# Four of the 32 groups of the samples' cache products on GpSimd and ScalarE, with a new plan, in a decoder layer on one Trainium2 core

## The chip, the core and the metric

The kernel runs on one core of one Trainium2 chip. The metric is the time of one execution on the device in microseconds (us). In the profile PE is TensorE's matrix products, PEld its weight loads, DVE VectorE, ACT ScalarE, POOL GpSimd, and SP SyncE, which issues most of the DMAs. L1223 is line 1223 of the kernel before; an arrow `a<-b` is read "a is written from b".

## What is computed

One step of a hybrid decoder layer for 1024 prompt tokens and 8 samples that share the weights, in float32, with model width 1024, 4 memory heads of width 256, and 256 memory rows. The part that matters here is the cross attention: the prompt attends to a memory whose keys and values are computed in the step, while each of the 8 samples attends to keys and values of its own, which are read from caches.

```python
def layer(x, ...):
    ...
    x = x + concat(pool_mixer(...), conv_mixer(...)) @ w_out
    x = x + cross_attn(rmsnorm(x, g_attn), mk, mv, w_q, w_o)
    h = rmsnorm(x, g_ffn)
    x = x + (silu(h @ w_gate) * (h @ w_up)) @ w_down

def cross_attn(h, k, v, w_q, w_o):
    q = (h @ w_q).reshape(B, L, MEM_HEADS, MEM_HEAD_DIM)
    s = einsum('blhd,bmhd->bhlm', q, k) / sqrt(MEM_HEAD_DIM)
    p = softmax(s, axis=-1)
    o = einsum('bhlm,bmhd->blhd', p, v).reshape(B, L, D_MODEL)
    return o @ w_o
...
xp, hp, cp = layer(xp, zp, zc, 0, mk, mv, *shared)
xs, hs, cs = layer(xs, state_pool[l], state_conv[l], PAST_LEN, cache_mem_k[l], cache_mem_v[l], *shared)
```

## The kernel before

Activations lie with channels on the 128 partitions and the 1024 + 8 = 1032 tokens as columns. Each float32 product is made of three passes: every operand is split into a high half and a residue, and high times high, high times residue and residue times high are summed. A split takes a copy to the rounded type (on ScalarE or GpSimd, L466 or L468) and a subtraction for the residue (on VectorE or GpSimd, L477). So each result that feeds another product costs two instructions on the engines beside TensorE; where the result comes from TensorE's output memory these are the evictions: a copy by ScalarE (L1188 for the value product) and the residue by VectorE (L1189).

The layer runs in stages: the input projections, pooling and convolution with the memory's keys and values (up to some 200 us), the output projection and queries (to 350 us), the attention of four heads (to some 425 us), its output projection `po` (L582), the gated feed-forward with `pr` (L1429) from some 524 us, and the down projection with the final norm.

In the attention stage a prompt block runs through scores `sc` (L1126), maximum and scaled exponential `probs` (L1134, L1136, L1143), normalising (L1151), a transpose `pt` to `pT` (L1165, L1169, L1170), and the value product `pv` into `oo` (L1184, L1188, L1189). `oo0` to `oo7` are the eight halves of the heads' outputs, the 8 sample columns of each included; `po` sums over them. A `po` block takes its 1032 columns in three spans of 344; the samples are the last columns of the last span.

Samples have a key and a value matrix each, so they get no matrix product with the cache: `s_dots` lays one head's query of all samples (`sbcache_k`, broadcast to 128 partitions by a DMA from the scratch `qd`) beside the cache (`spcache_k`), and VectorE multiplies 128x256 and sums it in one instruction for each sample (L1223). Four samples make a group, with one entry in the list of tasks. There are 32 groups: keys and values, 4 heads, 2 halves of 128, 2 sets of four samples. A group's number is 16 for values plus 4 times the head plus 2 times the half plus the set of samples. After a head's key groups come a transpose `ss` (L1236), a softmax on 8 rows (`sst`, `prow`), a DMA to the scratch `pd` and its broadcast `sbcache_v`; then the value groups sum into `qs`, whose halves are written into the sample columns of `oo` (L466 or L468, L477).

Nothing is issued in the order in which it is written. Each step is entered by `add` with the engines that may run it and a cost for each; `order` then plays through the engines, the buffers and the port that VectorE and GpSimd share, takes at each moment the step that can start first (within `SLACK`, by priority), and so fixes the sequence of each engine. `NUDGE` shifts the priority of single steps, `CHOSEN` binds a step to one engine, `LEAD` and `MARGINS` shift loads and costs. On the chip each engine then runs its sequence strictly in order, waiting for the others by semaphores.

Of the kernel before, what the change touches and what calls it, by code (L numbers as in the profile page):

```python
# [1986 lines left out]
```

## Time and profile before

| what | value |
|---|---|
| three runs | 1146.84, 1144.37, 1144.47 us; median 1144.47 us |
| the profiled execution | 1144.27 us |
| its span | 1142.5 us, so 1.8 us lie around it |
| granted TensorE clock, mean | 0.997 of full speed |
| busy: TensorE, VectorE, ScalarE, GpSimd | 1120.8, 927.6, 499.7, 287.8 us |

The busy time of a group of instructions doesn't say what it costs the whole; what ends an engine's idle time does. In a row of the groups by form the number behind x is the count, then stand the busy time in us and the mean of one in ns, and behind the second bar the idle time of that engine just before and what ended it. In a row of the timeline stand the start, the duration, engine, line, operation and operands, and in square brackets the idle time ahead of it with what ended it. Consecutive instructions of a form are joined with their count.

### The profile page before, as it was taken

The numbers are of one execution on the slowest core, as the hardware profiler recorded it, in microseconds if no ns is written. First come the engines' busy times: TensorE is split into PE (matmuls) and PEld (weight loads), VectorE is DVE, ScalarE is ACT, GpSimd is POOL, SyncE is SP. The second block draws the span as 40 slices with busy tenths as digits, with TensorE's granted clock in tenths as the row PEclk, the third lists the DMA queues.
The fourth block names the chain that finished last, engine by engine and source line by source line (L and its number), as shares of the span: only waits on it lengthen the run. The fifth ranks groups of instructions, "written<-read, shape, count | busy, mean of one in ns | idle before, by whom it ended". The sixth has DMA issues, their size and how long they took to land.

```text
span 1142.5 us, 19533 instructions
## 1 busy us (share of the span) xinstructions
PE 1120.8 (98%) x7736; PEld 1067.4 (93%) x7736; DVE 927.6 (81%) x1514; ACT 499.7 (44%) x706; POOL 287.8 (25%) x327
## 2 busy tenths in 40 slices
PE   9999999999999989999999999999999999999996
PEld 8999988999999979999999999999999999999996
DVE  7999999776257886888888888988888798879744
ACT  7766648353243452445233333333433443332444
POOL 2689772133712201433000000000000123332011
PEclk9999999999999999999999999999999999999999
DMA  8444587433485687322424352254433697657612
GB/s 307 94 93 110 127 233 237 163 114 149 165 249 176 207 325 244 123 82 75 140 84 149 128 190 105 100 176 159 156 124 112 237 374 286 242 169 235 186 59 91
DMA packets 66252, 193.54 MB, mean 169 GB/s; under 512 B 8368, under 2 KB 12144, under 8 KB 64880
## 3 DMA queue, kind: packets, MB, share of 16 engines
q1 hardware_dynamic: 62128, 178.81, 43.8%
q0 software_dynamic: 3600, 13.13, 6.6%
q8 instruction: 61, 1.00, 0.4%
q10 hardware_dynamic: 432, 0.36, 0.1%
q14 instruction: 31, 0.25, 0.1%
HBM read 147.84 MB, written 44.43 MB: 168 GB/s over the span
## 4 chain that ended last, share of the span: by engine, by line
PE 78%; DVE 15%; DMA 4%; issue 1%; ACT 1%; POOL 0%; DVEq 0%; SPq 0%; ACTq 0%; POOLq 0%
PE pr L1429 49%; PE po L582 7%; DVE cacc L783 6%; PE ps L582 5%; PE fd L1800 4%; PE oa L582 4%; PE ob L582 4%; DVE spcache_k L1223 1%; PE vps L1027 1%; DMA spcache_k<-in_cache_k 1%; PE kps L949 1%; PE pv L1184 1%; DVE spcache_v L1223 1%; DVE xss L513 1%; DVE x L1854 1%
## 5 line engine op out<-in xcount | busy, mean ns | idle before, releaser
L1429 PEld LDWEIGHTS pr<-ab,wTb 128*128 128x128 f32 x1056 | 123.4, 190 | 2.3 <-issue 0.5
L1429 PE MATMUL pr<-ab,wTa 128*128 128x260 f32 x1056 | 124.9, 275 | 0.0
L1429 PE MATMUL pr<-ab,wTb 128*128 128x260 f32 x1056 | 124.3, 275 | 0.0
L1429 PEld LDWEIGHTS pr<-ab,wTa 128*128 128x128 f32 x1056 | 123.1, 190 | 1.3
L1429 PE MATMUL pr<-ab,wG 128*128 128x512 f32 x528 | 121.1, 380 | 0.0
L1429 PEld LDWEIGHTS pr<-ab,wG 128*128 128x128 f32 x528 | 96.9, 189 | 12.5 <-issue 0.5
L582 PE MATMUL ps<-xop,w 128*128 128x344 f32 x720 | 105.5, 309 | 0.0
L582 PEld LDWEIGHTS ps<-xop,w 128*128 128x128 f32 x720 | 105.0, 189 | 0.0
L1445 DVE TENSOR_TENSOR su<-pr,su 128x520 f32<-128x520 f32 (+1 forms) x112 | 77.3, 692 | 25.9 <-PE pr L1429 25.4
L1429 PEld LDWEIGHTS pr<-hb,dV 128*128 128x128 f32 x768 | 92.3, 190 | 2.2
L1429 PE MATMUL pr<-hb,dV 128*128 128x260 f32 x768 | 92.7, 275 | 0.0
L582 PE MATMUL ps<-xq,w 128*128 128x344 f32 x576 | 87.0, 310 | 0.0
L582 PE MATMUL po<-oo,w 128*128 128x344 f32 x576 | 84.7, 309 | 0.0
L582 PEld LDWEIGHTS po<-oo,w 128*128 128x128 f32 x576 | 84.3, 189 | 0.2
L582 PEld LDWEIGHTS ps<-xq,w 128*128 128x128 f32 x576 | 84.2, 189 | 0.1
L783 DVE SCALAR_TENSOR_TENSOR cacc<-glu,vec,cacc 128x502 f32<-128x502 f32 (+14 forms) x116 | 77.5, 739 | 0.1
L1429 PE MATMUL pr<-hb,dW 128*128 128x512 f32 x288 | 69.2, 379 | 0.0
L1456 POOL MEMSET su<- 128x16 f32 x22 | 2.4, 112 | 255.7 <-PE pr L1429 200.1
L1800 PE MATMUL fd<-ho,w 128*128 128x260 f32 (+1 forms) x432 | 64.3, 311 | 0.0
L1800 PEld LDWEIGHTS fd<-ho,w 128*128 128x128 f32 x432 | 59.8, 190 | 4.4 <-issue 0.5
L1445 DVE TENSOR_TENSOR x<-pr,x 128x512 f32<-128x512 f32 (+1 forms) x76 | 52.3, 690 | 12.7 <-PE pr L1429 11.6
L766 POOL TENSOR_TENSOR y<-y,cp 128x511 f32<-128x511 f32 (+14 forms) x46 | 57.6, 1254 | 14.9 <-DVE y L766 7.2
(314 smaller groups left out, 2164.7 us busy)
## 6 DMA issues: line engine op xcount, KB each, us to landing
gr<-in_w_gu SPq DMA_DIRECT2D x44, 512.0 KB, 3.4
hb<-su SPq DMA_DIRECT2D x16, 520.0 KB, 3.8
hb<-hb SPq DMA_DIRECT2D x16, 520.0 KB, 6.7
dr<-in_w_dn SPq DMA_DIRECT2D x16, 512.0 KB, 4.0
hb<-bh SPq DMA_DIRECT2D x14, 520.0 KB, 3.3
hb<-hb SPq DMA_DIRECT2D x14, 512.0 KB, 7.4
spcache_k<-in_cache_k SPq DMA_DIRECT2D x12, 512.0 KB, 5.2
ho<-hd SPq DMA_DIRECT2D x10, 520.0 KB, 6.3
```

Of the source, the lines that this page charges most:

```text
L513: add({"Pool": pool_tt(n), "DVE": dve(n)}, lambda e: e.tensor_tensor(total(), total(), sq[:, i, :n], ALU.add), [(sq, i), tkey], [tkey], lo ...
L582: e.matmul(placed(ps[:, c, :CW]), w[:, wi, cols], turns(x[:, xi, c * CW : (c + 1) * CW]), start=first and p == 0, stop=last and p == 2)
L766: add({"Pool": pool_tt(HALF), "DVE": dve(HALF)}, lambda e: e.tensor_tensor(yb[:, i, HALF + n : SEQ], yb[:, i, HALF + n : SEQ], cp[:, q, : ...
L783: e.scalar_tensor_tensor(acc[h][:, n:], src[:, : HALF - n], w, acc[h][:, n:], ALU.mult, ALU.add)
L949: e.matmul(placed(ps[:, 0, i * NMEM : (i + 1) * NMEM]), w[:, wi, block_cols(k)], turns(memg[k // 4][:, xi, k % 4]), start=(k == 0 and p == ...
L1027: e.matmul(placed(ps[:, m]), memg[k // 4][:, xi, k % 4, m * P : (m + 1) * P], turns(w[:, wi, col : col + 512]), start=(k == 0 and p == 0), ...
L1184: e.matmul(placed(ps[:, c]), v[:, vi, m, col : col + P], turns(pT[h][m][:, pi, sl]), start=(m == 0 and p == 0), stop=(m == 1 and p == 2))
L1223: e.scalar_tensor_tensor(piece[:, b], piece[:, b], 1.0, bc[:, b], ALU.mult, ALU.mult, accum_out=out(m)[:, first + b : first + b + 1])
L1429: e.matmul(placed(bank(c)), w[:, wi, cols(j)], turns(xs[0](j, xi)[:, c * n : (c + 1) * n]), start=onto is None and j == 0 and p == 0, stop ...
L1445: from_sums(sums, "DVE", dve, lambda e, src, sl: e.tensor_tensor(as_banks(o(sl), src), src, as_banks(a(sl), src), op), [akey], [okey])
L1800: e.matmul(placed(view(i)), w[:, wi, col : col + P], turns(hops[k][:, xi, half, lo - half * HALF + i * width // count : lo - half * HALF + ...
L1854: add({"DVE": dve(n * width)}, lambda e, i=i, n=n: e.tensor_tensor(x2[j][:, i : i + n, sl], x2[j][:, i : i + n, sl], fin[:, sl].unsqueeze( ...
```

## The change

Four groups are named in `AWAY`. 13 and 15 are the second four samples of the last head's keys (halves 0 and 1), 29 and 31 those of its values. In them GpSimd multiplies all four samples in one 128x1024 instruction (`times`), and ScalarE sums each sample by a copy with an accumulator (`total`), four instructions. The other 28 groups stay on VectorE. The normalising of probabilities may now run on ScalarE too, and one value product (`pv4`) makes both its column halves before either is copied. All tables of the planner have new numbers, so the order moves all over the program. TensorE and SyncE have the same work as before. Line numbers in the kernel after are higher by about 85 to 110.

```diff
-LEAD = {"w_k": 4, "w_v": 7, "w_out_a": 16, "w_q": 42, "w_in": 22, "w_out_b": 11, "w_o": 14}
+LEAD = {"w_k": 4, "w_v": 7, "w_out_a": 10, "w_q": 34, "w_in": 16, "w_out_b": 12, "w_o": 14}
...
-DOWN_BY_DMA = (0, 0, 0, 4)
+DOWN_BY_DMA = (0, 0, 0, 3)
...
+AWAY = (13, 15, 29, 31)
+PV_MS = ()
+PV_FIRST = (4,)
 SCORES_MM = (5, 12, 13, 15)
-SLACK = {"Pool": 0.021, "ACT": 0.186, "DVE": 0.095, "PE": 0.044}
+SLACK = {"Pool": 0.02, "ACT": 0.109, "DVE": 0.058, "PE": 0.038}
...
 NUDGE = {
-    16: 148, 47: -35, 55: 6, 69: -37, 109: -90, 116: -39, 157: 141, 161: 1316, 177: 49, 178: 49, 179: 49, 180: 49, 181: 49, 182: 49,
+    16: -8, 22: -24, 32: 39, 44: -18, 50: -16, 51: 23, 55: -29, 57: -42, 69: -26, 88: 54, 93: 46, 99: 37, 100: -55, 103: -34, 109:
...
@@ normalise, in the softmax of the prompt's scores
         def normalise(e):
             for i in range(2):
-                e.tensor_scalar(pr[:, 2 * i2 + i], pr[:, 2 * i2 + i], st[:, 6 + i : 7 + i], 1.0, ALU.mult, ALU.mult)
-
-        add({"Pool": 0.95, "DVE": 0.53}, normalise, [(st, 2), (pr, i2)], [(pr, i2)], lock=True)
+                at, factor = pr[:, 2 * i2 + i], st[:, 6 + i : 7 + i]
+                if e is nc.scalar:
+                    e.activation(at, at, AF.Copy, scale=factor)
+                else:
+                    e.tensor_scalar(at, at, factor, 1.0, ALU.mult, ALU.mult)
+
+        add({"Pool": 0.95, "DVE": 0.53, "ACT": 2 * act(NMEM, ptrs=1)}, normalise, [(st, 2), (pr, i2)], [(pr, i2)], lock=True)
@@ pv
+        for step, c in ((matmuls, 0), (matmuls, 1), (copies, 0), (copies, 1)) if n in PV_FIRST else ((matmuls, 0), (copies, 0), (matmuls, 1), (copies, 1)):
+            step(c)
@@ s_dots
-                    add({"DVE": 1.4}, emit, [(piece,), (bc,)], [(piece, part), okey + (m, (first + part) // 4)], lock=True)
+                    dkey = okey + (m, (first + part) // 4)
+                    if number * 4 + m * 2 + (first + part) // 4 not in AWAY:
+                        add({"DVE": 1.4}, emit, [(piece,), (bc,)], [(piece, part), dkey], lock=True)
+                        continue
+
+                    def times(e, part=part, piece=piece, bc=bc):
+                        at = slice(part, part + 4)
+                        e.tensor_tensor(piece[:, at], piece[:, at], bc[:, at], ALU.mult)
+
+                    def total(e, m=m, first=first, part=part, piece=piece):
+                        for b in range(part, part + 4):
+                            e.activation(piece[:, b], piece[:, b], AF.Copy, accum_out=out(m)[:, first + b : first + b + 1])
+
+                    add({"Pool": pool_tt(1024)}, times, [(piece,), (bc,)], [(piece, part)], lock=True)
+                    add({"ACT": 4 * act(256) + 0.8}, total, [(piece, part)], [(piece, part), dkey])
```

The first place is VectorE at the last head's keys, second samples (`k3_0_4`, `k3_1_4`), where it makes the residues of `oo5`, `oo0` and `oo2` from the value products `pv` and those of the transposed probabilities `pT3`. Before:

```order
L1189 TENSOR_TENSOR oo5_4254<-pv5_4236,oo5_4254 128x512
L1223 SCALAR_TENSOR_TENSOR spcache_k3_0_4_4234,ssc_79<-spcache_k3_0_4_4234,sbcache_k3_4_4247 128x256 x4
L1189 TENSOR_TENSOR oo0_3726<-pv0_4283,oo0_3726 128x512
L1223 SCALAR_TENSOR_TENSOR spcache_k3_1_4_4252,ssc_79<-spcache_k3_1_4_4252,sbcache_k3_4_4247 128x256 x4
L1189 TENSOR_TENSOR oo2_3908<-pv2_4304,oo2_3908 128x512
L1244 TENSOR_REDUCE sst3_4331<-ss3_4327 8x1
L1245 SCALAR_TENSOR_TENSOR sst3_4331<-sst3_4331,r16_77 8x1
L1189 TENSOR_TENSOR oo0_3726<-pv0_4283,oo0_3726 128x512
L1170 TENSOR_TENSOR pT3_1_4279<-pt3_2_4294,pT3_1_4279 128x512
```

Now:

```order
L1283 TENSOR_TENSOR oo2_4059<-pv2_4229,oo2_4059 128x512
L1283 TENSOR_TENSOR oo5_4299<-pv5_4282,oo5_4299 128x512
L1257 TENSOR_TENSOR pT3_1_4277<-pt3_2_4294,pT3_1_4277 128x512
L1283 TENSOR_TENSOR oo0_3726<-pv0_4301,oo0_3726 128x512
L1283 TENSOR_TENSOR oo5_4299<-pv5_4282,oo5_4299 128x512
L1283 TENSOR_TENSOR oo0_3726<-pv0_4301,oo0_3726 128x512
L1257 TENSOR_TENSOR pT3_0_4237<-pt3_1_4324,pT3_0_4237 128x512
```

At the same place ScalarE makes the copies of these products; before, there stood only copies and the exponential `prow3` of the samples' softmax. Now:

```order
L1282 ACTIVATE oo5_4299<-pv5_4282 128x512
L1256 ACTIVATE pT3_1_4277<-pt3_2_4294 128x512
L1282 ACTIVATE oo0_3726<-pv0_4301 128x512
L1334 ACTIVATE spcache_k3_0_4_4220,ssc_79<-spcache_k3_0_4_4220 128x256 x4
L1282 ACTIVATE oo5_4299<-pv5_4282 128x512
L1282 ACTIVATE oo0_3726<-pv0_4301 128x512
L1334 ACTIVATE spcache_k3_1_4_4247,ssc_79<-spcache_k3_1_4_4247 128x256 x4
L1256 ACTIVATE pT3_0_4237<-pt3_1_4324 128x512
L1282 ACTIVATE oo6_4370<-pv6_4351 128x512
L1359 ACTIVATE prow3_4389,sst3_4379<-ss3_4367,sst3_4379,r16_77 8x256
```

The eight dots are gone from between VectorE's residues. On ScalarE the four sums of `k3_0` and of `k3_1` stand in front of the second copies of `oo5` and `oo0` and in front of the last copy to `pT3`.

The second place is TensorE at the end of the first two output blocks, `po0` and `po4`, where the samples' values are read (x9 is all three spans, x6 the first two, x3 the last, in which the samples are). Before:

```order
L582 MATMUL po0_4369<-oo7_4427,w44_4075 128x344 x6
L582 MATMUL po4_4491<-oo0_3726,w45_4005 128x344 x9
L582 MATMUL po4_4491<-oo1_3728,w45_4005 128x344 x9
L582 MATMUL po4_4491<-oo2_3908,w45_4005 128x344 x9
L582 MATMUL po4_4491<-oo3_3933,w45_4005 128x344 x9
L582 MATMUL po4_4491<-oo4_4132,w45_4005 128x344 x9
L582 MATMUL po0_4369<-oo6_4374,w44_4075 128x344 x3
L582 MATMUL po0_4369<-oo7_4427,w44_4075 128x344 x3
L582 MATMUL po4_4491<-oo5_4254,w45_4005 128x344 x9
L582 MATMUL po4_4491<-oo6_4374,w45_4005 128x344 x9
```

Now:

```order
L665 MATMUL po0_4359<-oo7_4459,w44_4077 128x344 x6
L665 MATMUL po4_4490<-oo0_3726,w45_4004 128x344 x3
L665 MATMUL po4_4490<-oo1_3877,w45_4004 128x344 x9
L665 MATMUL po4_4490<-oo2_4059,w45_4004 128x344 x9
L665 MATMUL po4_4490<-oo3_3999,w45_4004 128x344 x9
L665 MATMUL po4_4490<-oo4_4145,w45_4004 128x344 x9
L665 MATMUL po4_4490<-oo5_4299,w45_4004 128x344 x9
L665 MATMUL po4_4490<-oo6_4370,w45_4004 128x344 x6
L665 MATMUL po4_4490<-oo7_4459,w45_4004 128x344 x6
L665 MATMUL po0_4359<-oo6_4370,w44_4077 128x344 x3
L665 MATMUL po4_4490<-oo6_4370,w45_4004 128x344 x3
L665 MATMUL po0_4359<-oo7_4459,w44_4077 128x344 x3
```

The last spans of `oo6` and `oo7` have moved behind all other work of `po0` and `po4`.

The third place is GpSimd from the last head's probabilities on (`oo4` to `oo7`: the halves of the samples' columns). Before:

```order
L1151 TENSOR_SCALAR probs3_4077<-probs3_4077,sm3_2_4112 128x256 x2
L1151 TENSOR_SCALAR probs3_4077<-probs3_4077,sm3_1_4156 128x256 x2
L1151 TENSOR_SCALAR probs3_4077<-probs3_4077,sm3_3_4216 128x256 x2
L468 TENSOR_SCALAR oo4_4132<-qs_78 128x8
L477 TENSOR_TENSOR oo4_4132<-qs_78,oo4_4132 128x8
L477 TENSOR_TENSOR oo5_4254<-qs_78,oo5_4254 128x8
L468 TENSOR_SCALAR oo7_4427<-qs_78 128x8
L477 TENSOR_TENSOR oo7_4427<-qs_78,oo7_4427 128x8
```

Now:

```order
L1238 TENSOR_SCALAR probs3_4074<-probs3_4074,sm3_3_4191 128x256 x2
L1330 TENSOR_TENSOR spcache_k3_0_4_4220<-spcache_k3_0_4_4220,sbcache_k3_4_4240 128x1024
L1330 TENSOR_TENSOR spcache_k3_1_4_4247<-spcache_k3_1_4_4247,sbcache_k3_4_4240 128x1024
L551 TENSOR_SCALAR oo4_4145<-qs_78 128x8
L551 TENSOR_SCALAR oo5_4299<-qs_78 128x8
L560 TENSOR_TENSOR oo5_4299<-qs_78,oo5_4299 128x8
L1330 TENSOR_TENSOR spcache_v3_0_0_4194<-spcache_v3_0_0_4194,sbcache_v3_0_4462 128x1024
L1330 TENSOR_TENSOR spcache_v3_1_0_4289<-spcache_v3_1_0_4289,sbcache_v3_0_4462 128x1024
L560 TENSOR_TENSOR oo6_4370<-qs_78,oo6_4370 128x8
```

Four products of 128x1024 with the caches now stand between the probabilities and the columns of `oo6`. On VectorE the dots of `v3_0` and `v3_1` are x4 each where they were x8, and the residue of the weight `w44` stands ahead of the residue of `oo1`'s second half where GpSimd had it.

More of the change, by code (lines that the diff above doesn't have):

```diff
@@ L41 @@
 ORDER = (
[5 rows of a table removed]
[5 rows of a table added]
 )
-BY_DMA = {"w_in": (0, 3, 4, 6, 7, 9, 10, 11), "w_k": (2, 3, 5), "w_o": (4, 5, 6), "w_out_a": (1,), "w_out_b": (3,), "w_q": (4, 5, 6), "w_v": (0, 7), "w_dn": (18, 19), "w_dn2": (1,)}
+BY_DMA = {"w_in": (0, 1, 3, 4, 6, 7, 9, 10, 11), "w_k": (2, 3, 5), "w_o": (4, 5, 6), "w_out_a": (1,), "w_out_b": (3,), "w_q": (4, 5, 6), "w_v": (0, 7), "w_dn": (18, 19), "w_dn2": (1,)}
 WIDE = ("w_k", "w_v")
-LEAD = {"w_k": 4, "w_v": 7, "w_out_a": 16, "w_q": 42, "w_in": 22, "w_out_b": 11, "w_o": 14}
+LEAD = {"w_k": 4, "w_v": 7, "w_out_a": 10, "w_q": 34, "w_in": 16, "w_out_b": 12, "w_o": 14}
 LAST_SPANS = ((0, 512), (512, 260), (772, 260))
@@ L60 @@
 PE_FIXED, PE_COLUMN = 0.0135, 0.000417
+AWAY = (13, 15, 29, 31)
+PV_MS = ()
+PV_FIRST = (4,)
 SCORES_MM = (5, 12, 13, 15)
-SLACK = {"Pool": 0.021, "ACT": 0.186, "DVE": 0.095, "PE": 0.044}
+SLACK = {"Pool": 0.02, "ACT": 0.109, "DVE": 0.058, "PE": 0.038}
 MARGINS = {
     "early": {"PE": (0.93, 0.0), "DVE": (0.93, 0.0), "Pool": (1.01, 0), "ACT": (1.02, 0)},
-    "gated": {"Pool": (1.04, 0.04), "DVE": (1.01, 0.02), "PE": (0.95, 0.04), "ACT": (1.08, 0.06)},
+    "gated": {"Pool": (0.96, 0.04), "DVE": (1.01, 0.02), "PE": (0.95, 0.04), "ACT": (1.1, 0.04)},
     "down": {"DVE": (1.03, 0.103)},
-    "last": {"PE": (0.99, 0), "DVE": (1.02, 0.183)},
+    "last": {"PE": (1.08, 0), "DVE": (1.04, 0.243)},
 }
 NUDGE = {
[45 rows of a table removed]
[116 rows of a table added]
 }
@@ L120 @@
     "ACT": (
-        133, 179, 183, 207, 297, 502, 608, 660, 738, 907, 1374, 1406, 1578, 1617, 1647,
[4 rows of a table added]
     ),
     "DVE": (
-        26, 176, 404, 412, 477, 601, 609, 737, 745, 922, 1395, 1529, 2551, 2552, 2644, 2646,
[4 rows of a table added]
     ),
     "Pool": (
-        141, 184, 186, 198, 206, 388, 409, 415, 419, 520, 529, 539, 541, 555, 651, 654, 661, 664, 718, 719, 721, 725, 906, 1018, 1022,
-        1082, 1095, 1180, 1531, 1648, 2553,
[5 rows of a table added]
     ),
@@ L1174, in pv, with matmuls, emit, copies @@
         h, dt = n // 2, n % 2
-        ps = mm_buf(f"pv{n}", 2)
+        apart = [ms_buf(f"pv{n}_{c}") for c in range(2)] if n in PV_MS else []
+        ps = None if apart else mm_buf(f"pv{n}", 2)
         col, v = (h % 2) * 256 + dt * P, vv[h // 2]
         oo = oop[n]
-        for c in range(2):
+        at = lambda c: apart[c] if apart else ps
+        bank = lambda c: apart[c][:] if apart else ps[:, c]
+        def matmuls(c):
             sl = slice(c * 512, (c + 1) * 512)
-            def emit(e, c=c, sl=sl):
+            def emit(e):
                 for m in range(2):
                     for p, (vi, pi) in enumerate(PASSES):
-                        e.matmul(placed(ps[:, c]), v[:, vi, m, col : col + P], turns(pT[h][m][:, pi, sl]),
+                        e.matmul(placed(bank(c)), v[:, vi, m, col : col + P], turns(pT[h][m][:, pi, sl]),
                                  start=(m == 0 and p == 0), stop=(m == 1 and p == 2))
-            add({"PE": pe(512, 6)}, emit, [(v, 0), (v, 1)] + [(pT[h][m], p, c) for p in range(2) for m in range(2)], [(ps,)])
-            add({"ACT": act(512, True)}, lambda e, c=c, sl=sl: e.activation(halves(oo[:, 0, sl]), drawn(ps[:, c]), AF.Copy), [(ps,)], [(oo, 0, c)])
-            add({"DVE": dve(512)}, lambda e, c=c, sl=sl: e.tensor_tensor(halves(oo[:, 1, sl]), drawn(ps[:, c]), halves(f32(oo[:, 0, sl])), ALU.subtract),
-                [(ps,), (oo, 0, c)], [(oo, 1, c)])
+            add({"PE": pe(512, 6)}, emit, [(v, 0), (v, 1)] + [(pT[h][m], p, c) for p in range(2) for m in range(2)], [(at(c),)])
+        def copies(c):
+            sl = slice(c * 512, (c + 1) * 512)
+            add({"ACT": act(512, True)}, lambda e: e.activation(halves(oo[:, 0, sl]), drawn(bank(c)), AF.Copy), [(at(c),)], [(oo, 0, c)])
+            add({"DVE": dve(512)}, lambda e: e.tensor_tensor(halves(oo[:, 1, sl]), drawn(bank(c)), halves(f32(oo[:, 0, sl])), ALU.subtract),
+                [(at(c),), (oo, 0, c)], [(oo, 1, c)])
+        for step, c in ((matmuls, 0), (matmuls, 1), (copies, 0), (copies, 1)) if n in PV_FIRST else ((matmuls, 0), (copies, 0), (matmuls, 1), (copies, 1)):
+            step(c)
     def s_query(h):
```

182 rows, old and new, of tables (CHOSEN, NUDGE, ORDER) are left out of this document.

## The prediction

> **What bounds the kernel now.** I read the page first, then busy time by stretches, then the waits of TensorE, and only then single instructions.
>
> ```profile
> span 1142.5 us, 19533 instructions
> ...
> PE 1120.8 (98%) x7736; PEld 1067.4 (93%) x7736; DVE 927.6 (81%) x1514; ACT 499.7 (44%) x706; POOL 287.8 (25%) x327
> PE 78%; DVE 15%; DMA 4%; issue 1%; ACT 1%; POOL 0%; DVEq 0%; SPq 0%; ACTq 0%; POOLq 0%
> ```
>
> TensorE is busy for 1120.8 of 1142.5 us and its list of work is the same after the change, so all that can be won is part of the 21.7 us in which it idles. The stretches show where (columns: us, then busy time and instructions of PE, PEld, DVE, ACT, POOL, then granted clock, DMA share, GB/s):
>
> ```profile
> 375.00:400.00 25.00, 24.08 (x172) 22.52 (x171) 21.80 (x77) 12.38 (x28) 6.30 (x8) 1.00 0.65 201
> 400.00:425.00 25.00, 21.88 (x121) 17.73 (x120) 21.05 (x69) 13.64 (x31) 2.82 (x6) 1.00 0.89 322
> 425.00:450.00 25.00, 25.00 (x166) 24.57 (x165) 18.12 (x73) 6.28 (x10) 2.55 (x8) 1.00 0.71 265
> 525.00:1075.00 550.00, 550.00 (x3928) 521.32 (x3927) 475.83 (x669) 199.72 (x256) 52.43 (x90) 1.00 0.49 174
> ```
>
> From 425 to 1075 us TensorE never idles: relief for another engine is worth nothing there, and any wait added there counts in full. The stage of the cached groups, up to 425 us, lacks 0.92 + 3.12 = 4.04 us. The waits of TensorE say on whom (us in total, times, longest):
>
> ```profile
> PE pv L1184 <- DVE oo L1189: 2.5, 4, 1.5
> PE vps L1027 <- DVE kf L953: 1.9, 1, 1.9
> PE sc L1126 <- ACT probs L1143: 1.6, 1, 1.6
> PE pt L1165 <- DVE pT L1170: 0.9, 1, 0.9
> PE kps L949 <- DVE a L935: 0.9, 1, 0.9
> PE Rx_ps L612 <- DVE xss L513: 0.9, 1, 0.9
> ```
>
> The first row is what the change aims at: the value product `pv` waits four times for VectorE's eviction `oo`. The worst case, TensorE first, then VectorE in the same microseconds:
>
> ```profile
> 417.63 1.56 PE L1184 MATMUL pv<-pT,vv 128*128 128x512 f32 x6 [1.48 <-DVE oo L1189]
> 419.03 0.38 PE L1236 MATMUL ss<-ident,ssc 128*8 128x128 f32 x2
> 419.61 1.56 PE L1184 MATMUL pv<-pT,vv 128*128 128x512 f32 x6 [0.20 <-DVE oo L1189]
> ...
> 421.36 1.54 PE L1184 MATMUL pv<-pT,vv 128*128 128x512 f32 x6
> ```
>
> ```profile
> 415.50 0.42 DVE L1223 SCALAR_TENSOR_TENSOR spcache_k<-spcache_k,sbcache_k 128x256 f32<-128x256 f32 x1 [1.02 <-DMA sbcache_k<-qd]
> ...
> 416.89 0.68 DVE L1189 TENSOR_TENSOR oo<-pv,oo 128x512 fp32r<-128x512 f32 x1
> ...
> 418.87 0.68 DVE L1189 TENSOR_TENSOR oo<-pv,oo 128x512 fp32r<-128x512 f32 x1
> ```
>
> VectorE stands idle for 1.02 us until the broadcast query lands; four dots follow, then an eviction, four more dots, an eviction. TensorE waits 1.48 and 0.20 us for them. These eight dots are two of the four groups that leave VectorE.
>
> **The change, part by part.** Prices, from the groups by form (count, busy us, mean ns):
>
> ```profile
> L1223 DVE SCALAR_TENSOR_TENSOR spcache_k<-spcache_k,sbcache_k 128x256 f32<-128x256 f32 x64 | 23.0, 420 | 8.7 <-DMA sbcache_k<-qd 5.7 <-DMA spcache_k<-in_cache_k 3.0
> L477 POOL TENSOR_TENSOR w<-raw,w 128x1024 fp32r<-128x1024 f32 x19 | 46.6, 2482 | 28.8 <-ACT w L466 28.3
> L477 DVE TENSOR_TENSOR w<-raw,w 128x1024 fp32r<-128x1024 f32 x14 | 18.9, 1348 | 0.6 <-ACT w L466 0.6
> L1143 ACT ACTIVATE probs<-sc,sm,r 128x256 f32<-128x256 f32 x32 | 17.7, 560 | 25.8 <-DVE sm L1136 13.5 <-DVE spcache_k L1223 7.4 <-PE sc L1126 4.5
> ```
>
> and two of ScalarE's exponentials with their sum, one behind the other:
>
> ```profile
> 399.36 0.55 ACT L1143 ACTIVATE probs<-sc,sm,r 128x256 f32<-128x256 f32 x1
> 399.80 0.19 ACT L1143 ACTIVATION_READ_ACCUMULATOR probs<-sc,sm,r 128x1 f32 x1
> 399.89 0.56 ACT L1143 ACTIVATE probs<-sc,sm,r 128x256 f32<-128x256 f32 x1
> ```
>
> A group of four dots holds VectorE from 415.50 to 416.89, 1.39 us. The same group elsewhere: one 128x1024 product on GpSimd, 2.48 us by the mean of the nearest form, and four sums of 128x256 on ScalarE. The trace shows no plain copy with a sum; the nearest is the exponential with one: 0.56 us, its read 0.44 us after its start, the next 0.53 after it. So four take 1.8 us (4 x 0.44, if a read cost nothing) to 3.0 (4 x 0.75, if nothing overlapped). I take 4 x 0.53 = 2.1, as here, because the four stand back to back. A group thus becomes 2.5 + 2.1 = 4.6 us of latency instead of 1.4, but off VectorE.
>
> (a) *Last head's keys, second half.* Eight dots leave VectorE's evictions. The four waits on `oo`, 2.5 us, lie between 405 and 420 us and are all fed by its backlog: **-2.5**, if nothing else holds the evictions. What is late next is ScalarE: it copies each `pv` first, and its sums stand in order between those copies. The broadcast landed at 415.50; the products would end at 418.0 and 420.5, the sums at 420.1 and 422.6, and the second `oo5` and `oo0` copies stand behind the first sum. TensorE's seventh product began at 421.4, so I cost this at nothing, and up to +2.5 (the gain lost) where the broadcast lands no sooner.
>
> (b) *The residue of weight w44* moves from GpSimd to VectorE, ahead of `oo1`: 1.35 us there. VectorE is busy for 21.80 of 25 us in that stretch. Bounds 0 and +1.35; taken halfway, **+0.6**, since idle and busy stretches alternate there.
>
> (c) *Last head's values, second half*: the long path. Its rows:
>
> ```profile
> 421.73 0.29 SPq L443 DMA_DIRECT2D pd<-prow  x1
> ...
> 427.62 0.32 SPq L443 DMA_DIRECT2D sbcache_v<-pd  x1
> ...
> 435.50 0.42 DVE L1223 SCALAR_TENSOR_TENSOR spcache_v<-spcache_v,sbcache_v 128x256 f32<-128x256 f32 x1 [1.23 <-DMA sbcache_v<-pd]
> ...
> 441.58 0.20 POOL L477 TENSOR_TENSOR oo<-qs,oo 128x8 fp32r<-128x8 f32 x1
> ```
>
> From the score transpose `ss3` (419.03, above) to the landed broadcast it is 16.5 us, to the finished sample columns of `oo7` 22.8 us. What TensorE does meanwhile is priced by two steps of the chain of waits:
>
> ```profile
> 422.91 1.75 PE po L582 x12
> 424.66 1.29 PE pv L1184 x6
> ```
>
> Before: 30 pv and 114 po matmuls and a transpose lie between `ss3` and the first matmul that reads those columns: 6.5 + 16.6 + 1.1 = 24.2 us, so 1.4 us to spare. In the new order `ss3` stands behind six `pv6` and six `po0` matmuls, and between it and that reader are 18 pv and 132 po: 3.9 + 19.3 = 23.1 us, although the sample spans are moved to the end of `po0` and `po4`. The new path is 16.5 to landing, two products 5.0 one after the other, sums 2.1, the two halves of the split 0.5: 24.1 us. That is **+1.0** of wait. Bounds: 0, as `ss3` now comes 3 us later while the cache loads around it don't, so the broadcast may cross a quieter queue (it took 7.9 us from issue); and +5.4, if the products also wait for VectorE's eight remaining dots (2 x 1.39 = 2.8) and for one more 516 KB load of `xa` ahead of the broadcast (1.6 us at the 322 GB/s of the 400 to 425 row).
>
> The rows that bear on this last bound are these three:
>
> ```profile
> 354.31 2.36 POOL L477 TENSOR_TENSOR w<-raw,w 128x1024 fp32r<-128x1024 f32 x1
> 354.84 1.84 DVE L1136 SCALAR_TENSOR_TENSOR sm<-sm,r 128x2 f32<-128x2 f32 x1
> ...
> 394.50 0.16 DVE L1136 SCALAR_TENSOR_TENSOR sm<-sm,r 128x2 f32<-128x2 f32 x1
> ```
>
> A VectorE instruction of two elements takes 0.16 us alone and 1.84 beside a GpSimd product, and ends when that product ends (356.68 and 356.67). [...]
>
> (d) *Elsewhere.* The normalising of probabilities moves in part to ScalarE and residues move between VectorE and GpSimd, with the work behind them in the same order to within a few rows: 0, between -1 and +1, by the 1.9 and 0.9 us of the `vps` and `kps` waits, whose VectorE order stays. The start runs value weights ahead of gate weights; the wait `Rx_ps` (0.9) ends on VectorE anyway and covers it: 0 to +0.9. Past 525 us nothing can be gained; a replanned order may lose up to 1.
>
> Sum: -2.5 + 0 + 0.6 + 1.0 + 0 = -0.9. The profiled execution took 1144.27 us (span 1142.5 and 1.8 around it), so 1143.4; the median shown is 0.2 higher, so **1143.6 us**: no difference that a measurement can tell, since that begins at about 0.2%, 2.3 us.
>
> **The rivals.**
>
> *The relief pays in full.* The broadcast of (c) lands sooner, w44's residue falls into VectorE's idle time, and the other gaps of the stage shrink too. Between -2.5 and -4.0 (all idle time from 375 to 425): 1140.5 to 1142.0, say 1141.2. For it: four waits name VectorE. Against it: VectorE's idle 1.02 us just ahead of the dots shows that the query's DMA ends last there, and a DMA isn't made faster.
>
> [...]
>
> *ScalarE takes VectorE's place.* Copies of `oo5` and `oo0` wait behind sums that wait for GpSimd; the gain of (a) goes: 1143.6 + 2.5 = 1146.1, still within 0.2% of before. For it: the order itself, and a group that takes 4.6 us where it took 1.4. Against it: two `pv` buffers are open in turn, so a copy may be late by one product.
>
> *It doesn't do what it says* hardly applies: the order shows the four products on GpSimd and 16 sums on ScalarE.
>
> **How the numbers follow.** Forecast 0.35, relief in full 0.32, ScalarE in VectorE's place 0.12, late values 0.21. Faster 0.32, same 0.35 + 0.12 = 0.47, slower 0.21. The range takes in -4.0 at the low end (1140.5, and 0.7 for (d)) and the late values with part of (d) at the high end: 1139.8 to 1148.0; the forecast's own range is 1142.2 to 1145.5, its (b) and (c) between nothing and 3.5 together.
>
> **What would show it.** (a) is right if the waits of `pv` on `oo` fall under 0.5 us and TensorE's busy time from 400 to 425 us rises by some 2; wrong if ScalarE's `oo` copies start later than the products that they read have ended, with the sums ahead of them. (b) shows as a wait of `pt` or `pv` on VectorE near 385 to 392 us. [...] The forecast is wrong if TensorE now idles past 525 us, or in the 142 to 151 us stretch by over 1 us more or less than 2.8.

## The result and the profile after

The changed kernel takes **1151.44 us** (median of 5 runs, 1150.83 to 1153.19), the kernel before 1144.47 (5 runs beside it, 1142.87 to 1146.84): a ratio of **1.006, 95% interval 1.0046 to 1.0074**. It is slower by 7 us where 0.9 us less was forecast, and lies above the forecast's range. Two later measurements of the unedited changed kernel, on other chips, gave 1.0081 (1.0066 to 1.0096) and 1.009 (1.0075 to 1.0105).

The page of the profiled execution, span, busy time and the engines' shares of the chain that ended last:

```profile
span 1149.2 us, 19578 instructions
...
PE 1123.3 (98%) x7736; PEld 1070.8 (93%) x7736; DVE 931.5 (81%) x1492; ACT 497.1 (43%) x729; POOL 298.1 (26%) x330
PE 76%; DVE 12%; issue 5%; DMA 4%; POOL 2%; ACT 1%; ACTq 0%; DVEq 0%; POOLq 0%
```

TensorE's 7736 matmuls are the same, yet they are busy for 2.5 us more, and its idle time has grown from 21.7 to 25.9 us. The work is unchanged, so this is a slower clock: the granted clock is 0.994 of full speed on average, 0.997 before. The waits of TensorE name the largest new wait (us in total, times, longest):

```profile
PE kps L1032 <- DMA w<-in_w_k: 5.7, 1, 5.7
PE psv L665 <- POOL w L551: 2.2, 1, 2.2
PE sc L1209 <- ACT probs L1226: 2.0, 1, 2.0
PE pv L1275 <- DVE oo L1283: 1.4, 3, 0.6
...
PE po L665 <- DVE xa L1406: 1.0, 1, 1.0
PE sq L1295 <- DVE qs L1190: 0.8, 1, 0.8
PE ss L1347 <- DVE pT L1257: 0.7, 1, 0.7
```

To see where the 7 us arise, read the first and last start of TensorE's work on a tile ("29.8 to 31.2"), of before and then of after:

```profile
L612 PE MATMUL Rx_ps<-xss,ones_n x4: 593/593/667, 29.8 to 31.2; 128*128 128x512 f32 x4
L949 PE MATMUL kps<-memg,w x192: 272/275/533, 137.7 to 192.4; 128*128 128x256 f32 x192
L1126 PE MATMUL sc<-kT,qo x192: 272/275/377, 329.0 to 404.6; 128*128 128x256 f32 x192
L1184 PE MATMUL pv<-pT,vv x96: 379/379/483, 389.1 to 432.5; 128*128 128x512 f32 x96
L582 PE MATMUL po<-oo,w x576: 309/309/309, 422.7 to 510.5; 128*128 128x344 f32 x192
```

```profile
L695 PE MATMUL Rx_ps<-xss,ones_n x4: 592/592/592, 31.0 to 32.3; 128*128 128x512 f32 x4
L1032 PE MATMUL kps<-memg,w x192: 273/275/581, 138.8 to 196.7; 128*128 128x256 f32 x192
L1209 PE MATMUL sc<-kT,qo x192: 272/275/377, 333.7 to 409.4; 128*128 128x256 f32 x192
L1275 PE MATMUL pv<-pT,vv x96: 379/379/483, 395.3 to 438.0; 128*128 128x512 f32 x96
L665 PE MATMUL po<-oo,w x576: 309/309/413, 426.2 to 516.4; 128*128 128x344 f32 x192
```

The lag is 1.1 us at the end of the start (31.2 to 32.3), 4.3 at the last key (192.4 to 196.7), 4.7 at the first score, 5.5 at the last `pv`, 5.9 at the last `po`, and 6.7 at the end of the span. Of these, 3.2 us (1.1 to 4.3) arise among the keys of the memories, far from the four groups. The timeline there (start us, us, engine, line, what it does; in brackets the wait ahead of it):

```profile
136.34 0.89 POOL L578 DMA_DIRECT2D w<-in_w_k  x1
136.79 0.35 SPq L526 DMA_DIRECT2D raw<-in_w_k  x1
...
138.82 0.38 PE L1032 MATMUL kps<-memg,w 128*128 128x256 f32 x2
...
144.88 1.43 PE L1032 MATMUL kps<-memg,w 128*128 128x256 f32 x5 [5.67 <-DMA w<-in_w_k]
```

The new order has the eight steps of `kps1` ahead of `kps0`. The low half of the weight of `kps1` is written by GpSimd's accumulating transfer, issued at 136.34; the third product needs it and waits until 144.88, 8.5 us after that issue. In the kernel before, `kps0`, whose weights were there, filled that time. The granted clock falls to 0.50 during the wait (0.81 from 142 to 143 us, then 0.50) and stays there up to 149 us, for the work behind it (columns: us, busy time of PE and its matmuls, granted clock, DMA share, GB/s):

```profile
139.00:142.00 3.00, 0.21 (x2) 1.00 1.02 251
142.00:146.00 4.00, 1.12 (x5) 0.58 0.97 226
146.00:150.00 4.00, 4.00 (x23) 0.57 0.76 195
150.00:154.00 4.00, 4.00 (x38) 1.00 0.77 213
```

23 products are done from 146 to 150 us at a granted clock of 0.57, where 38 are done in the next 4 us at 1.00: the wait costs a second time, as slow work.

### The profile page after: what moved, and what is told of

It is laid out like the page before. It is cut to its first block, busy times and chain, and to the rows that moved or that the text cites. A ratio compares the mean times of both kernels' runs of the same rounds, so it can differ in the third digit from the quotient of the medians.

```text
span 1149.2 us, 19578 instructions
## 1 busy us (share of the span) xinstructions
PE 1123.3 (98%) x7736; PEld 1070.8 (93%) x7736; DVE 931.5 (81%) x1492; ACT 497.1 (43%) x729; POOL 298.1 (26%) x330
## 4 chain that ended last, share of the span: by engine, by line
PE 76%; DVE 12%; issue 5%; DMA 4%; POOL 2%; ACT 1%; ACTq 0%; DVEq 0%; POOLq 0%
PE pr L1540 48%; PE po L665 7%; PE ps L665 6%; DVE cacc L866 5%; PE fd L1911 4%; PE ob L665 4%; PE oa L665 3%; DVE spcache_k L1320 1%; PE psv L665 1%; PE psg L665 1%; DMA spcache_k<-in_cache_k 1%; DMA w<-in_w_out_a 1%; PE pv L1275 1%; DVE spcache_v L1320 1%; DVE x L1965 1%
## 5 line engine op out<-in xcount | busy, mean ns | idle before, releaser
L665 PE MATMUL ps<-xop,w 128*128 128x344 f32 x720 | 105.5, 309 | 0.0
L1540 PE MATMUL pr<-ab,wU 128*128 128x512 f32 x264 | 60.6, 379 | 0.0
```

Source lines behind the costliest of these rows:

```text
L665: e.matmul(placed(ps[:, c, :CW]), w[:, wi, cols], turns(x[:, xi, c * CW : (c + 1) * CW]), start=first and p == 0, stop=last and p == 2)
L1540: e.matmul(placed(bank(c)), w[:, wi, cols(j)], turns(xs[0](j, xi)[:, c * n : (c + 1) * n]), start=onto is None and j == 0 and p == 0, stop ...
```

## The experiments

Most kernels here run the steps of the plan from a written list, so that single steps can stand elsewhere; their lines stand some 36 to 50 further down. The diffs show the steps by engine and tile. "Ratio" is to the kernel before, timed beside the run.

**First group: which part of the new order costs.**

```diff
 e1_early: changed kernel, every step planned ahead of 190 us
-  in the new order
+  in the order of before
```


> The kernel after, with its steps up to the last key product (some 190 us) put back into the order of before; the attention stage with the four groups on GpSimd and ScalarE, and all that follows, stay as after. Theory A (the time was lost in the early stages, which the new plan moved too: +1.1 us at the start, +3.1 us where TensorE takes kps1 ahead of kps0 and waits for a weight half): about 1147.2 us, 2.7 us over before, and no TensorE wait on w<-in_w_k. Theory B (the four groups themselves cost it, by the shared port and by ScalarE's sums ahead of its copies): about 1151, as after.


Ratio 1.0044 (1.0028 to 1.0061): Theory A in its direction only. The early lag was gone, but a wait of 3.0 us for `spcache_k` near 352 us, which neither profile above has, hid what that is worth. It can't be put down to the edit: c2_before, the kernel before on the same chip, has one of 2.2 us.

```diff
 e2_kps: changed kernel
-PE kps1 x8, kps0 x16
+PE kps0 x15, kps1 x8, kps0 x1
```


> The kernel after with one swap: TensorE's 15 steps of kps0 stand ahead of the 8 steps of kps1 again, as before. Theory A: about 1148.3 us, 3.1 us less than after, the wait of 5.7 us for w<-in_w_k gone and matrix products at full speed behind it. Theory A with another cause (the weight half lands late because GpSimd issues its DMA late, so that the wait only moves): over 1150. Theory B: 1151.


Ratio 1.0055 (1.0037 to 1.0073), hardly below the changed kernel's, where Theory A had 3.1 us less. The wait was gone and the keys ended 4.3 us earlier than in the profile of after, but a larger one stood near 450 us:

```profile
453.16 3.28 PE L701 MATMUL po<-oo,w 128*128 128x344 f32 x15 [3.25 <-DVE xa L1442]
```

```profile
449.51 1.23 DVE L1442 TENSOR_TENSOR xa<-po,xa 128x1032 f32<-128x1032 f32 x1 [3.87 <-PE po L701]
450.66 1.22 DVE L596 TENSOR_TENSOR w<-raw,w 128x1024 fp32r<-128x1024 f32 x1
451.79 1.23 DVE L1442 TENSOR_TENSOR xa<-po,xa 128x1032 f32<-128x1032 f32 x1
```

That was the edit's own doing: turning two buffers had put `po1` into the bank of `po4`, which the second addition frees at 453.02, instead of that of `po0`, which the first one frees. It shows what the 1.0 us wait of the changed kernel is: a wait for an output bank.

```diff
 e3_dots_back: changed kernel
-POOL product 128x1024 x4, ACT sum x16
+DVE dot x16
```


> The kernel after in its own order, but the four groups run on VectorE again, each where GpSimd's product stood; ScalarE's sums are gone. Theory A: no gain, 1151.4 to 1153 us, since VectorE's evictions wait for the dots again and TensorE's early waits stay. Theory B: under 1149 us.


Ratio 1.0084 (1.0064 to 1.0104), but many buffers stood in other turns than in the changed kernel, so this run alone decides nothing.

```diff
 e4_attention: kernel before, steps planned from 351 to 440 us
-  in the order of before
+  in the new order, with the four groups
```


> The kernel before, with only its attention stage (from some 355 to 450 us, up to the first two output blocks) in the order of after, the four groups on GpSimd and ScalarE there. Theory A: 1145.7 us, 1.2 us over before, most of it the 1.0 us that TensorE waits for VectorE's addition of po0 because po0 and po4 now end together. Theory B: 1149 to 1151 us. If the relief of VectorE pays, under 1144.


Ratio 1.012 (1.010 to 1.0141). Here too `po1` had the wrong bank (a wait of 4.0 us, to the end of the second addition), but that is 4.0 of 13.7 us. From the first `sc` to the last `pv` the run takes 112.3 us, the kernel before 103.5, with waits of 2 to 3 us for `spcache_k`, `probs` and `qs`. Neither theory foresaw this size. Other buffers moved here too, and c2_before has the wait for `spcache_k`, so how much of it is the order stays open.

**Second group: three causes apart.** From here on every later buffer keeps its turn; where an edit exchanges two buffers, they stay exchanged to the end.

> The changed kernel itself, unedited, so that the other runs of this group have its trace from the same chip. Both theories: 0.4 to 0.8% slower than the kernel before, with the 5.7 us wait of the first keys, a wait of about 1 us of the output product for VectorE's addition to xa near 452 us, and waits of about 2 us for probs. If the wait for spcache_k near 350 us is 3 us here too, and the wait of pt near 385 us about 2 us, then those waits of the earlier runs belong to the chip and not to their edits.


Ratio 1.0081 (1.0066 to 1.0096), median 1155.67 us; the waits of 3 us at `spcache_k` did not recur, a wait of 1.1 us of `pt` for probabilities did.

```diff
 e5_kps_clean: changed kernel, buffers behind it unmoved
-PE kps1 x8, kps0 x16
+PE kps0 x15, kps1 x8, kps0 x1
```


> The changed kernel with only the two groups of key products of the memories turned back (kps0 ahead of kps1), and, unlike e2_kps, every later buffer in the bank that it has in the changed kernel. Theory one (the loss is in what the new order moved, and the two mistimed places add up): the 5.7 us wait goes, products end 3.4 us earlier from there on, the wait of po for xa stays near 1.0 us (3.3 in e2_kps was the bank), so the time is 2.5 to 3.5 us below c1_after. Theory two (later waits for data that comes by its own time take it back): 0 to 1 us below c1_after.


Ratio **1.0035** (1.002 to 1.005), 1149.56 us: 6.1 us below c1_after, more than either theory said. In the traces 3.8 us are won by the end of the first output projection (243.3 to 239.5), the other 3 in the attention stage; over half of those is the clock, below.

```diff
 e6_po_turn: changed kernel
-PE po4<-oo7, po0<-oo6 (samples), po4<-oo6 (samples), po0<-oo7 (samples), po4<-oo7 (samples)
+PE po0<-oo6 (samples), po0<-oo7 (samples), po4<-oo7, po4<-oo6 (samples), po4<-oo7 (samples)
```


> The changed kernel with only five products of the output projection in another order: the sample columns of oo6 and oo7 of po0 ahead of the last three of po4, so that po0 ends 1.7 us before po4. Theory one (the wait near 452 us is for a free output bank, which VectorE's addition of po0 to xa frees): the wait of 1.0 us goes, nothing comes in its place, the time is 0.7 to 1.1 us below c1_after. Theory two (samples are late): a wait on ScalarE's or VectorE's oo comes at the moved products, 0 to 2 us, and the time is the same as c1_after or above.


Ratio 1.0067 (1.0053 to 1.0082): 2.2 us below c1_after by the medians, though the intervals overlap. The trace decides: the 1.0 us wait is gone and no wait for samples has come, 70 products in one piece:

```profile
447.75 10.47 PE L701 MATMUL po<-oo,w 128*128 128x344 f32 x70
```

```diff
 e7_fill: changed kernel, in keys(q), first step of kps1
+if q == 1 and i == 0 and k == 0 and p == 0:
+    for n in range(48):
+        e.matmul(placed(ps[:, 0, NMEM : 2 * NMEM]), ready[0][:, 0, block_cols(n % 8)], turns(memg[0][:, 0, n % 4]),
+                 start=True, stop=True)
```


> The changed kernel with 48 further products of 128x256 on weights that are there already, issued ahead of kps1's first product, into the bank that kps1 then writes anew; their result is not used. They take about 5.1 us of the 5.7 us wait. Theory one (half of the cost of a wait of that length is the clock: the products behind it ran at 0.25 us instead of 0.107 for some 6 us): granted clock stays near 1 in 142 to 152 us, products behind it at 0.107 us from the start, the time 2.0 to 3.0 us below c1_after although the weight is as late as before. Theory two (only the wait costs; the slow products are not from the pause): time the same as c1_after within 0.5 us.


Ratio 1.0048 (1.003 to 1.0066), 4.5 us below c1_after. The weight is as late as before, but TensorE is kept busy, and the granted clock stays at 1.00:

```profile
139.00:142.00 3.00, 3.00 (x30) 1.00 1.03 253
142.00:146.00 4.00, 3.85 (x35) 1.00 1.02 236
146.00:150.00 4.00, 4.00 (x39) 1.00 0.75 174
```

39 products where the changed kernel has 23. The profiled executions lie only 1.9 us apart. In them the keys end 2.8 us earlier than in c1_after, 0.7 of it from the start, so the place is worth some 2.1 us, as theory one said; what the rest of the 4.5 us is, isn't shown.

The same program also showed a second place of this kind. At 361 us `sc` waits 1.95 us for `probs`, in the profile of after and in c1_after alike; the work behind it, after first:

```profile
362.88 1.60 PE L1209 MATMUL sc<-kT,qo 128*128 128x256 f32 x12 [1.95 <-ACT probs L1226]
364.32 2.79 PE L665 MATMUL ps<-xq,w 128*128 128x344 f32 x18
```

```profile
363.13 1.81 PE L1209 MATMUL sc<-kT,qo 128*128 128x256 f32 x12 [1.95 <-ACT probs L1226]
364.74 4.29 PE L665 MATMUL ps<-xq,w 128*128 128x344 f32 x18
```

```profile
364.00:365.00 1.00, 1.00 (x8) 0.69 0.31 118
365.00:366.00 1.00, 1.00 (x5) 0.50 0.01 5
366.00:367.00 1.00, 1.00 (x5) 0.50 0.03 12
367.00:368.00 1.00, 1.00 (x6) 0.60 0.89 365
```

One execution loses 1.7 us behind the wait, the other nothing. In e5_kps_clean the wait there is 1.7 us, and the granted clock stayed at 1.00.

**Third group: the parts alone, in the kernel before.**

> The kernel before, unedited, for its trace on the same chip as the other runs of this group. Every theory: the same time as the kernel before within 0.3%, no wait of the first keys, one pause of about 2.1 us between the keys and the values near 150 us with the clock at half for 4 us behind it, no pause above 1.9 us between 160 and 525 us.


One run, 1145.42 us, as the kernel before.

```diff
 e8_groups_alone: kernel before
-DVE dot x16
+POOL product 128x1024 x4, ACT sum x16 (behind them)
```


> The kernel before in its own order, with nothing of the change but the four groups: their four multiplications stand on GpSimd where VectorE's dots stood, their sums on ScalarE behind them, and what must wait for the sums stands behind those. Theory one (the groups help as the prediction had it, the rest of the new order costs): 0 to 3 us below the kernel before, the waits of pv for VectorE's oo near 405 to 420 us shrink from 2.5 us by 1 to 2. Theory two (the groups themselves cost, by GpSimd's two slow multiplications beside VectorE's dots, by ScalarE's sums and by the scores of the samples that come later): 0.5 to 3 us above it, with waits at ss, at pT or at the samples' columns of oo.


Ratio **1.0048** (1.003 to 1.0066): theory two. TensorE, near 421 us:

```profile
421.52 0.27 PE L1303 MATMUL ss<-ident,ssc 128*8 128x128 f32 x1
423.10 0.27 PE L1303 MATMUL ss<-ident,ssc 128*8 128x128 f32 x1 [1.31 <-ACT spcache_k L1290]
426.05 3.78 PE L621 MATMUL po<-oo,w 128*128 128x344 f32 x12 [2.67 <-DVE oo L1239]
```

The waits of `pv` shrink from 2.3 to 1.1 us, as hoped, but the scores are ready 3 us later than by VectorE's dots (`ss3` read both halves at 420.14 in c2_before), and what follows stands behind them, on ScalarE and VectorE too. Behind the second wait 12 products take 3.78 us instead of 1.91, at a granted clock of 0.50 (426 to 430 us): half the clock again. Of the 6.4 us between the two profiled executions, 5.0 are there at the last `po`; the other 1.4 come near 1127 us, where TensorE waits 1.8 us for GpSimd's `fin` (0.3 in c2_before).

```diff
 e9_keys_first: kernel before
-PE kps0 x15, kps1 x8, kps0 x1
+PE kps1 x8, kps0 x16
```


> The kernel before with one thing of the change: the 24 steps of the products of the first two groups of keys in the changed kernel's order (kps1 ahead). Theory one (this place is where most of the loss is): a wait of about 5 us for the weight's low half and half the clock for 6 us behind it appear, the pause near 150 us goes; 2.5 to 4 us above the kernel before, and up to 2 more where a later pause of some 2 us crosses into the half clock. Theory two (the loss is in the attention stage alone): within 1 us of the kernel before.


Ratio 1.0007 (0.9991 to 1.0023): by the time theory two, 0.8 us above the kernel before. The wait and the half clock of theory one appeared (0.52 from 142 to 144 us), but the wait was shorter,

```profile
142.57 1.65 PE L985 MATMUL kps<-memg,w 128*128 128x256 f32 x6 [3.36 <-DMA w<-in_w_k]
```

6.2 us after the transfer's issue (136.33) instead of 8.5, and the 1.9 us wait of `vps` for `kf`, with the half clock behind it, was gone in exchange (granted clock 1.00 from 150 to 158 us).

```diff
 e10_three_undone: changed kernel
+steps of the first 16 us as before, keys as in e5_kps_clean, output as in e6_po_turn
```


> The changed kernel with three places turned back: the steps of the first 16 us (without the loads of later weights) and the order of the first two groups of keys as before, and the five products of the output projection as in e6_po_turn. The four groups stay on GpSimd and ScalarE. Theory one (these three places carry the loss, 1.1 + 3.4 to 6 + 1.0 us of it): 5.5 to 9 us below the changed kernel of c1_after as a ratio to the kernel before, that is a ratio of 0.999 to 1.003. Theory two (the attention stage in its new order costs by itself): the ratio stays above 1.004.


Ratio 1.0035 (1.0021 to 1.0049), neither theory; in the profiled run the first `psv` waited 3.0 us and the first stage ended 2.0 us later than in e14_two_undone below; the attention stage, too, was longer (107.8 us beside 105.5).

**Fourth group: groups, clock, start, sum.**

```diff
 e11_dots_back_clean: changed kernel, buffers unmoved
-POOL product 128x1024 x4, ACT sum x16
+DVE dot x16
```


> The changed kernel with the four groups back on VectorE, each run of four dots where the multiplication stood, and, unlike e3_dots_back, every buffer in the turn that it has in the changed kernel; the order of all other steps is the changed kernel's. Theory one (in the new order the groups on GpSimd and ScalarE save VectorE's time where PE waits for it; the loss is in the places that moved): 1 to 5 us above the changed kernel, that is a ratio of 1.0085 to 1.012 where the changed kernel has 1.006 to 1.008. Theory two (the groups themselves cost, as in e8_groups_alone, and e3 was slower by its buffers): 1 to 5 us below the changed kernel, a ratio of 1.002 to 1.005.


Ratio 1.0084 (1.007 to 1.0098). The changed kernel has 1.006 to 1.009: in the new order the groups neither gain nor cost by a size that these times can tell. From the first `sc` to the last `pv` this run takes 108.9 us, the changed kernel 104.3 and 108.1 in two executions at full clock, and 108.5 in c1_after, 1.7 of it lost to the clock.

```diff
 e12_before_fill: kernel before, in values(c), first step of vps1
+for n in range(16 if c == 1 and k == 0 else 0):
+    e.matmul(placed(spare[1][:, 2, :NMEM]), memg[0][:, 0, n % 4, :P], turns(memg[0][:, 0, (n + 1) % 4]), start=True, stop=True)
```


> The kernel before with 16 further products of 128x256, 1.7 us of work, ahead of the first product of the values, where TensorE stands still for 2.1 us near 150 us and then runs at half the clock for 4 us; they write an unused bank and their result is not used. Theory one (a pause of 2.1 us ends at half the clock, one of under 1.9 us does not): granted clock 1.0 in 152 to 156 us, the values' products 1.8 to 2.2 us earlier, the time 1 to 2.2 us below the kernel before, ratio 0.998 to 0.999. Theory two (the slow products have another cause): no change within 0.5 us.


Ratio 1.0011 (1.0001 to 1.0021), neither theory's time: the granted clock stayed at 1.00 from 152 to 156 us (0.63 in c2_before) and the twelve products of `vps` took 2.83 us instead of 4.52, but waits for VectorE took the time back:

```profile
PE pmap L1012 <- DVE win L962: 1.0, 1, 1.0
...
PE kps L991 <- DVE kf L995: 0.4, 1, 0.4
```

The half clock was gone with the pause, but nothing was gained: the 1.7 us won went into waits for VectorE.

```diff
 e13_start_as_after: kernel before
+steps of the first 16 us in the new order (psv ahead of psg)
```


> The kernel before with the first 16 us of steps in the changed kernel's order (psv ahead of psg, the loads of the first weights and inputs with them), nothing else. Theory one (the new order of the start costs): products of the first stage end 1.0 to 1.3 us later (31.0 us where the kernel before has 29.2 to 29.8), a pause of over 2 us ahead of the first psv, the time 0.8 to 1.4 us above the kernel before. Theory two (the start differs by when the first loads land, run by run): same as the kernel before within 0.5 us.


Ratio 1.0003 (0.9993 to 1.0014): theory two by the time. The trace has what theory one said, a pause of 2.1 us ahead of the first `psv` and the first stage over a microsecond later than in the profile of before; but e9_keys_first, with the old start, shows a first stage as late, so the landing of the first loads decides as much as the order.

```diff
 e14_two_undone: changed kernel
+keys as in e5_kps_clean, output as in e6_po_turn
```


> The changed kernel with the keys' order of e5_kps_clean and the output projection's order of e6_po_turn together. Theory one (the two places add up, 0.46% and 0.1 to 0.2% of the time): a ratio of 1.0015 to 1.003, what is left being the start (about 1.1 us) and the attention stage's waits for probs and qs (about 1 us). Theory two (e5 had gained by chance in the attention stage, where its pause of 1.8 us stayed below what halves the clock): a ratio of 1.0035 to 1.005.


Ratio **1.002** (1.0009 to 1.0032), theory one. Keys and output bank carry most of the loss. From the first `sc` to the last `pv` it takes 105.5 us, as e5_kps_clean; the kernel before 103.5, 105.2 in c2_before, and 104.2 in e13_start_as_after.

**Fifth group: why the weight is late.**

```diff
 e15_loads_back: changed kernel
-SP raw<-in_w_k, wmap, raw<-in_w_v
+SP wmap, raw<-in_w_v, raw<-in_w_k
```


> The changed kernel with one load of a key weight (raw<-in_w_k, 512 KB, which the changed kernel issues 0.45 us behind GpSimd's accumulating transfer for the weight of kps1) moved back to where the kernel before has it, behind the map of the pooling and the next load of a value weight, and its high half on ScalarE with it; the keys' products stay in the changed kernel's order. Theory one (kps1's weight is late because that load shares the transfers with it: e9_keys_first, whose loads stand as before, waits 3.4 us where the changed kernel waits 4.9 to 5.8): the wait of kps for the weight falls to 3.0 to 3.8 us, half the clock behind it stays for one stretch of some 3.4 us instead of two, the first keys end 2 to 4 us earlier, the time 2 to 4 us below c3_after. Theory two (GpSimd's transfer takes its 8.5 us whatever is issued beside it): wait 5 to 6 us, time within 1 us of c3_after, or above it where w16 comes late.

> The changed kernel unedited, for its time and trace on the same chip. Every theory: 0.5 to 0.8% slower than the kernel before, with a wait of 4.9 to 5.8 us of kps for the weight.


e15: 1.007 (1.0054 to 1.0086), c3: 1.009 (1.0075 to 1.0105). The wait was 5.3 us beside 6.0 in c3_after, not 3.0 to 3.8, and the weight was read 8.2 us after its issue, as in c1_after: the neighbouring load is not what makes the weight late. The median lies 2.4 us below c3_after, as theory one had it, but the intervals overlap. Why the weight could be read 6.2 us after issue in e9_keys_first and 8.2 to 8.9 in the others stays open.

No variant beats the kernel before; e13_start_as_after and e9_keys_first equal it.

## Why the prediction was wrong

**The step that failed is (d), "elsewhere", costed at 0 between -1 and +1.** It read the order of the keys from VectorE's side ("whose VectorE order stays") and took the work behind as standing "in the same order to within a few rows". It doesn't mention that `kps1` and `kps0` trade places on TensorE, and they are not alike: `kps1` reads a weight whose low half a transfer of GpSimd still had to bring. The trace of before has when GpSimd issued it, and when `kps1` first ran, behind 45 products of `kps0`:

```profile
135.25 0.90 POOL L495 DMA_DIRECT2D w<-in_w_k  x1
...
143.78 5.93 PE L949 MATMUL kps<-memg,w 128*128 128x256 f32 x51 [0.88 <-DVE a L935]
```

So this trace shows the weight to be there only 8.5 us after its issue. The wait measured 5.7 us in place of the 0.9 and 1.9 that went. The clock, which the step did not price at all, took another 2.1 (e7_fill), less the 1.7 that it had taken behind the 1.9 us wait before (e12_before_fill). Together that is 3.3 us; the lag of the keys is 3.2. Undone alone (e5_kps_clean) the swap gives back 6.1 of the 9.9 us that the changed kernel lost on that chip, more than this place by itself. The text had named the place as one to watch: 142 to 151 us, off by over 1 us.

**(a) was right in its place, under half its size, and was taken back.** The waits of `pv` on `oo` fell from 2.5 to 1.4 us, not under 0.5, and TensorE's busy time from 400 to 425 us rose by 0.95 us (21.88 to 22.83), not by 2. The longest of these waits shows the sign that the text gave for (a) being wrong: ScalarE's copy of `oo` starts right behind its sums, 1.0 us after the products that it reads have ended (422.47), and TensorE waits for the residue behind that copy:

```profile
423.06 0.40 ACT L1334 ACTIVATE spcache_k<-spcache_k 128x256 f32<-128x256 f32 x1
...
423.46 0.58 ACT L1282 ACTIVATE oo<-pv 128x512 fp32r<-128x512 f32 x1
...
424.07 1.48 DVE L1283 TENSOR_TENSOR oo<-pv,oo 128x512 fp32r<-128x512 f32 x2 [1.54 <-ACT oo L1282]
...
424.82 1.56 PE L1275 MATMUL pv<-pT,vv 128*128 128x512 f32 x6 [0.62 <-DVE oo L1283]
```

What it set against that, at nothing up to +2.5, was latency: alone, the groups cost 5.5 us (e8_groups_alone), most of it because two products and eight sums in a row bring the scores 3 us later. In the new order, where other work stands ahead of the scores, they cost nothing that shows (e11_dots_back_clean), but that order pays with waits that were not there: `sq` for `qs` 0.8, `ss` for `pT` 0.7. The stage came out 0.8 us longer in the profiled pair instead of 0.9 shorter for the whole kernel, and 4.6 us longer in another at full clock (c3_after, 108.1 beside 103.5).

**(b) cost nothing that shows**: no wait of `pt` or `pv` on VectorE stands between 385 and 392 us in the profile of after. But the residue of `w44` doesn't stand there; VectorE makes it from 402.45 to 403.67 us, and behind it TensorE works on without a wait until 407.18, where `pt` waits 0.49 us for ScalarE's `probs`.

**(c) named the wrong end.** The path is as described, but shorter: the broadcast landed 12.5 us after `ss3` (427.09) instead of 16.5, and the sums took 0.40 us each instead of 0.53. VectorE's last dots:

```profile
439.64 0.41 DVE L1320 SCALAR_TENSOR_TENSOR spcache_v<-spcache_v,sbcache_v 128x256 f32<-128x256 f32 x1
...
439.98 2.58 DVE L1320 SCALAR_TENSOR_TENSOR spcache_v<-spcache_v,sbcache_v 128x256 f32<-128x256 f32 x1
...
442.48 2.58 DVE L1320 SCALAR_TENSOR_TENSOR spcache_v<-spcache_v,sbcache_v 128x256 f32<-128x256 f32 x1
```

GpSimd starts its two products at 439.63 (5.15 us for both), along with VectorE's first dot, and the next two dots take 2.58 us each beside them, where that first one and those behind take 0.41. The columns of `oo7` are ready at 447.76, 20.7 us after `ss3` instead of 24.1, and the reader comes near 451: no wait for samples. No run shows the late values that the range's high end counts in and that had a chance of 0.21; in their place the trace has these two long dots and columns that are ready 3 us ahead of their reader. The 1.0 us of (c) came all the same, from what (c) moved: with the sample spans at the end of both, `po0` and `po4` finish together, and `po1` finds no free bank until VectorE has added `po0` (451.89, 1.23 us). e6_po_turn removes it. The number was right by chance.

**The start** ("0 to +0.9") measured +0.3 us, with an interval of -0.8 to +1.6 (e13_start_as_after); the profiled pair differs there by 1.1.

The rivals missed it as well: each was about the four groups, and none about another place that the new plan had moved. ScalarE in VectorE's place came true in small, in the 0.6 us wait above.

**What stays open.** The same swap of keys in the kernel before costs only 0.8 us (-1.0 to +2.6, e9_keys_first), because the weight is there 6.2 us after its issue: the swap hurts together with the late weight, and why that is later in the changed kernel isn't shown. The attention stage isn't settled either. It takes 104.3, 108.5 and 108.1 us in three executions of the unedited changed kernel, so one profile doesn't tell what an edit did there; its new order takes 112.3 us in the kernel before (e4_attention, with moved buffers), and 105.5 with keys and output turned back (e14_two_undone).

## What to carry to other kernels

When a planner runs anew, price the whole difference of order, above all where TensorE's own steps trade places: for each moved step look up when its last operand lands, low halves and accumulated parts too. Taking work off a busy engine lengthens its path (the scores came 3 us later in e8_groups_alone); ask who waits for the result before counting the relief. Price a wait of TensorE with the clock behind it: here the clock cost 1.7 us behind waits of 1.9 us (before) and 1.95 us (c1_after), nothing behind waits of 1.95 us (after) and 2.97 us (e4_attention), and some 2.1 us behind the one of 5.7 us. Filling the wait paid in e7_fill; in e12_before_fill, where other waits stood right behind, it didn't.

## What the hardware showed unexpectedly

The clock fell to half for 3.4 us in some executions and for twice that in others. In the last view of c1_after above the half clock covers 0.62 of the first us, two whole, and 0.80 of the last: 3.4 us. Before has 3.4 us as well, from 152 to 156 us (0.58, 0.50, 0.50, 0.71), behind its wait of 1.9 us. In after it lasts two such lengths, 6.8 us (142 to 150 us in the view of the keys, at 0.58 and 0.57), and begins inside the 5.7 us wait. A wait of 1.95 us was followed by it in c1_after, the same wait in after was not, and in e4_attention one of 2.97 us (up to 353.41) was followed by the full clock (1.00 from 353 to 358 us). What decides this isn't shown. So the same program loses or keeps 1.7 us from one execution to the next, which is part of why executions of one kernel differ by some us here.
